# Second score pass of two attention layers on all 128 array rows, with a new table of priorities

## The chip, the cores and the metric

One core of a Trainium2 chip runs the whole program. The time is the device time of one execution in microseconds (us). The kernel before was timed three times: 1111.57, 1105.31 and 1106.12 us, median 1106.12 us.

## The reference

Four layers run one after the other on 512 tokens of 1024 channels, each as a pre-normalised residual: differential attention (layer 0), a gated causal convolution of 31 taps (layer 1), latent attention with a low-rank query and key (layer 2), differential attention again (layer 3). Cut to the scores, which the change touches:

```
# layers 0 and 3: 8 heads, two score maps (m = 0, 1) per head, 64 channels each
s = einsum('bhmqd,bhmkd->bhmqk', q[:, :, :, s0:e], k[:, :, :, :e]) * scale
p = chunk_causal_softmax(s, s0)
wts = p[:, :, 0] - lam * p[:, :, 1]
outs.append(einsum('bhqk,bhkd->bhqd', wts, v[:, :, :e]))
# layer 2: 8 heads, 128 channels without rotation and 64 rotated ones, the rotated key shared by all heads
s = (einsum('bhqd,bhkd->bhqk', qn[:, :, s0:e], kn[:, :, :e])
     + einsum('bhqr,bkr->bhqk', qr[:, :, s0:e], k_rope[:, :e])) * scale
```

Queries are taken in four blocks of 128 tokens, and block j sees the keys of blocks 0 to j.

## The kernel before

**Precision.** Every large product is made of float32r passes. An operand is split exactly into a high and a low part, and a product is the sum of high by high, high by low and low by high (`mm3`, three matmuls into the same PSUM bank).

**Scores of layers 0 and 3.** A map has only 64 channels, so one 128-row plane holds the high part of the query on one half of the partitions and its low part on the other (`stack`). The key tile has five planes of 512 tokens: 0 and 1 are the query's for m = 0 and 1, 2 and 3 hold the high part of the key of m = 0 and 1, copied to both halves, and plane 4 holds the low parts, that of m = 0 on the first 64 partitions, that of m = 1 on the last 64. A score block is then two passes: a first with 128 rows, (high and low query) by high key, and a second with the 64 rows of one half, high query by low key. Where the query block sees fewer than 256 keys, 256 are computed.

**Scores of layer 2.** Three passes with 128 rows for the unrotated channels, one with 128 rows for the rotated ones by the high key, and one with 64 rows for the rotated ones by the low key. The rotated key already stands on both halves of the partitions, its high and its low part.

**Around a score block.** VectorE masks it and takes the row maximum, ScalarE takes the exponential, TensorE transposes the weights (`wtr`), ScalarE copies them out (`wt`), TensorE multiplies them with V (`o`). One head follows the other; the projections of the next heads (`qk_a`, `v_a`, `g_a`, `q_a`, `kv_a`) and the output projection (`o` from `o_w` and `y`) stand between them on TensorE.

**Making a head ready (layers 0 and 3).** TensorE transposes query and key (`qk_tr`), ScalarE casts them into the head's tile `st` (six casts of 64 partitions), VectorE subtracts to get the low parts (four subtractions of 64 partitions).

**What sets the order.** The program is recorded as nodes, one engine each. `Plan.order` takes them by a list schedule: for each engine the node that could start first by estimated costs, ties by priority. Priority is the place in the program, shifted by the table `SHIFT` (one number for each section and engine) and by `AS` for attention. Buffers are slots counted in `SLOTS` and PSUM tiles are granted while the order is made. Each engine then runs its list strictly in that order, with semaphore waits. All loads are issued by SyncE.

In names of the profile the numbers are left out (`L_qk_st` is `L0_qk3_st1`, for example), so layers 0 and 3 share names.

Of the kernel before, what the change touches and what calls it, by code (L numbers as in the profile page):

```python
# [248 lines left out]
L1_ab6_w.pool=-54 L1_ab6_w_r.sp=4 L1_c0.dve=672 L1_c1.dve=701 L1_c3.dve=765 L1_c5.dve=1250 L1_c7.pe=185
L1_cq2.act=741 L1_cq2.pool=293 L1_cq4.act=-380 L1_cq4.pool=-367 L1_cs0.act=-348 L1_cs5.act=60 L1_cs6.act=-31  # L250
L1_cs7.act=3 L1_ct2_.act=94 L1_ct4_.act=-5138 L1_ctr0.act=123 L1_ctr0.pe=4634 L1_ctr1.act=-1571 L1_ctr1.pe=566
L1_ctr2.act=494 L1_ctr2.pe=492 L1_ctr3.act=809 L1_ctr3.pe=24 L1_ctr4.act=-1038 L1_ctr4.pe=-1038 L1_ctr5.act=852
# [1300 lines left out]
```

## Time and profile before

| | |
|---|---|
| median of three runs | 1106.12 us (1105.31 to 1111.57) |
| profiled execution, first to last instruction | 1108.7 us |
| TensorE matmul busy | 1065.0 us (96%), 5089 instructions |
| TensorE weight load busy | 847.5 us (76%) |
| VectorE busy | 813.3 us (73%) |
| ScalarE busy | 623.6 us (56%) |
| GpSimd busy | 209.5 us (19%) |
| DMA | 78.16 MB, mean 70 GB/s |

The page shows no time of its own for the profiled execution beside its span. A matmul's busy time reaches from its start to a modelled end and overlaps with the next, so "busy" on TensorE is not the same as productive: how far apart the starts of successive matmuls are says more. In rows of the trace, "64\*128" after the operation is rows by columns of the array that were used, and "128x512" is the moving operand. The layers lie at about 0 to 323, 323 to 556, 556 to 810 and 810 to 1109 us.

### The profile page before, as it was taken

What the parts mean: (1) busy time and instruction counts of PE and PEld (TensorE: products, weight loads), DVE (VectorE), ACT (ScalarE), POOL (GpSimd) and SP (SyncE); (2) the same over time, 40 slices, a digit from 0 to 9 for tenths busy, and PEclk for the clock granted to TensorE, in tenths of its full rate; (3) what the DMA queues carried; (4) which work ended last, traced back from release to release, by engine and by line L of the source; (5) the groups of instructions that cost most, each with busy time, mean ns of one, the idle gap of its engine ahead of it and who ended that gap; (6) DMA issues with size and microseconds to landing.
All of it is one profiled execution on the core that took longest, in us unless ns stands there. A gap on an engine that the chain in (4) does not pass through costs nothing.

```text
span 1108.7 us, 15142 instructions
## 1 busy us (share of the span) xinstructions
PE 1065.0 (96%) x5089; PEld 847.5 (76%) x5089; DVE 813.3 (73%) x2271; ACT 623.6 (56%) x1319; POOL 209.5 (19%) x133
## 2 busy tenths in 40 slices
PE   8899999999998998898999999999999999999898
PEld 6777877777686786686888877888887787777677
DVE  3876688888754999988555878874775588878771
ACT  6466366657654355796444676654435645667652
POOL 2400000000027499985520000000300000000000
PEclk9999999999999998999999999999999999999899
DMA  7231220302013322202231311011423121212002
GB/s 225 78 94 58 77 77 20 117 22 95 20 39 114 113 78 76 69 1 92 56 109 46 93 53 39 20 56 58 136 93 94 59 77 58 79 55 77 1 20 76
DMA packets 67254, 78.16 MB, mean 70 GB/s; under 512 B 15813, under 2 KB 44741, under 8 KB 67176
## 3 DMA queue, kind: packets, MB, share of 16 engines
q1 hardware_dynamic: 67176, 77.19, 22.7%
q8 instruction: 40, 0.66, 0.2%
q14 instruction: 38, 0.31, 0.1%
HBM read 75.08 MB, written 2.10 MB: 70 GB/s over the span
## 4 chain that ended last, share of the span: by engine, by line
PE 82%; DVE 5%; ACT 4%; POOL 3%; issue 2%; DMA 1%; SPq 1%; POOLq 0%; DVEq 0%; ACTq 0%
PE L_o L451 20%; PE L_qk_a L451 14%; PE L_g_a L451 13%; PE L_v_a L451 8%; PE L_ab_a L451 5%; PE L_c L451 2%; POOL L_cq L502 2%; POOL L_sqs L502 1%; PE L_q_a L451 1%; PE L_h6j_sc L451 1%; PE L_h1j_sc L451 1%; PE L_h5j_sc L451 1%; PE L_h4j_sc L451 1%; PE L_h7j_sc L451 1%; PE L_h3j_sc L451 1%
## 5 line engine op out<-in xcount | busy, mean ns | idle before, releaser
L451 PE MATMUL L_qk_a<-L_qk_w,Hh 128*128 128x512 f32 x512 | 164.1, 401 | 2.7 <-ACT Hh L481 1.9
L451 PE MATMUL L_o<-L_y,L_o_w 128*128 128x512 f32 x576 | 141.9, 397 | 1.2 <-DVE L_y L499 1.0
L502 POOL TENSOR_TENSOR L_sqs<-L_sqs,L_sq 128x512 f32<-128x512 f32 x28 | 44.2, 1579 | 513.2 <-DMA L_lay<-c_q_norm_g 275.9
L451 PE MATMUL L_g_a<-L_g_w,Hh 128*128 128x512 f32 x384 | 123.8, 404 | 0.7 <-DVE L_c_v L514 0.6
L451 PEld LDWEIGHTS L_o<-L_y,L_o_w 128*128 128x128 f32 x576 | 105.4, 188 | 24.3 <-DVE L_y L499 1.4
L451 PEld LDWEIGHTS L_qk_a<-L_qk_w,Hh 128*128 128x128 f32 x512 | 92.4, 188 | 24.0 <-ACT Hh L481 2.3
L506 DVE SCALAR_TENSOR_TENSOR L_c<-L_u,L_tab,L_c 128x512 f32<-128x512 f32 x150 | 102.8, 746 | 0.3
L451 PE MATMUL L_qk_a<-L_qk_w,Hl 128*128 128x512 f32 x256 | 100.3, 392 | 1.3 <-DVE Hl L506 1.3
L451 PE MATMUL L_ab_a<-Hh,L_ab_w 128*128 128x512 f32 x256 | 81.7, 397 | 0.7 <-DVE L_u L499 0.7
L451 PE MATMUL L_v_a<-L_v_w,Hh 128*128 128x512 f32 x256 | 81.7, 400 | 0.0
L451 PEld LDWEIGHTS L_g_a<-L_g_w,Hh 128*128 128x128 f32 x384 | 68.5, 189 | 16.9 <-issue 2.0
L502 POOL TENSOR_TENSOR L_cq<-L_cq,L_ct 128x512 f32<-128x512 f32 x60 | 79.4, 1323 | 10.5 <-ACT L_ct L481 7.2
L451 PE MATMUL L_g_a<-L_g_w,Hl 128*128 128x512 f32 x192 | 75.2, 392 | 0.0
L488 ACT CAST L_qk_st<-L_qk_tr 64x512 fp32r<-64x512 f32 x96 | 55.7, 580 | 15.5 <-PE L_qk_tr L457 14.3
L451 PEld LDWEIGHTS L_ab_a<-Hh,L_ab_w 128*128 128x128 f32 x256 | 48.8, 191 | 11.4 <-DVE L_u L499 1.1
L451 PEld LDWEIGHTS L_qk_a<-L_qk_w,Hl 128*128 128x128 f32 x256 | 48.1, 188 | 12.0 <-DVE Hl L506 1.7
L481 ACT ACTIVATE L_ct<-L_u,L_tab 128x512 f32<-128x512 f32 x60 | 43.0, 719 | 23.5 <-POOL L_cq L502 23.3
L451 PEld LDWEIGHTS L_v_a<-L_v_w,Hh 128*128 128x128 f32 x256 | 46.2, 188 | 10.0 <-issue 0.9
L451 PE MATMUL L_ab_a<-Hl,L_ab_w 128*128 128x512 f32 x128 | 50.6, 395 | 1.4 <-DVE Hl L506 1.4
L488 ACT CAST L_qk_w<-L_qk_w_r 128x1024 fp32r<-128x1024 f32 (+1 forms) x33 | 34.2, 1039 | 31.1 <-PE L_qk_a L451 15.3
L451 PE MATMUL L_g_a<-Hh,L_g_w 128*128 128x512 f32 x128 | 46.1, 415 | 5.4 <-POOL L_g_w L502 2.6
L451 PE MATMUL L_o<-L_o_w,L_y 128*128 128x512 f32 (+1 forms) x216 | 50.5, 379 | 0.5 <-DVE L_y L506 0.5
(376 smaller groups left out, 2387.1 us busy)
## 6 DMA issues: line engine op xcount, KB each, us to landing
L_qk_w_r<-a_w_in SPq DMA_DIRECT2D x62, 256.0 KB, 3.0
L_v_w_r<-a_w_in SPq DMA_DIRECT2D x16, 512.0 KB, 3.7
L_g_w_r<-a_w_in SPq DMA_DIRECT2D x16, 512.0 KB, 3.7
L_o_w_r<-a_w_out SPq DMA_DIRECT2D x16, 512.0 KB, 3.5
L_ab_w_r<-b_w_in SPq DMA_DIRECT2D x24, 256.0 KB, 3.0
L_g_w_r<-b_w_in SPq DMA_DIRECT2D x8, 512.0 KB, 3.7
L_o_w_r<-b_w_out SPq DMA_DIRECT2D x8, 512.0 KB, 3.5
L_g_w_r<-c_w_in SPq DMA_DIRECT2D x8, 512.0 KB, 3.6
```

Of the source, the lines that this page charges most:

```text
L451: lambda nc: nc.tensor.matmul(out.real(), a.real(), b.real(), start=start, stop=stop),
L481: nc.scalar.activation(out.real(), src.real(), func, scale=scale.real() if isinstance(scale, View) else scale, **kw)
L488: lambda nc: nc.scalar.copy(out.real(), src.real()), [src], [out])
L502: lambda nc: nc.gpsimd.tensor_tensor(out=out.real(), in0=a.real(), in1=b.real(), op=op), [a, b], [out])
L506: self.add("dve", out.n / 960.0 + (0.13 if isinstance(scalar, View) else 0.068), lambda nc: nc.vector.scalar_tensor_tensor(out=out.real(), ...
```

## The change

The second score pass of layers 0, 2 and 3 uses all 128 rows: the whole query plane (high and low part) by the low part of the key, which now stands on both halves of the partitions. It adds the product low by low, which was left out before. In layers 0 and 3 the low parts of the two maps get a plane each (tile `qk` with six planes instead of five, four slots), and two ScalarE copies of 64 partitions per head bring each low part to the other half. In layer 2 only the index changes. The number of matmuls and their moving sizes stay.

`build` asks for a DMA scratch of 1024 instead of the default. In the planner the estimated cost of a matmul is a little larger, and VectorE instructions whose operands all lie in SBUF are reckoned to be held up by a busy GpSimd (`port`). The table of priorities is another one: 875 entries instead of 883, most numbers differ. Comments are gone. The new table reorders every engine's list.

```diff
 SLOTS = {
...
-    "qk": (4, [P, 5, 512], F32R, True),
+    "qk": (4, [P, 6, 512], F32R, True),
...
 SHIFT = {k: int(v) for k, v in (x.split("=") for x in """
...
-L3_ytr3.pe=-303 L3_ytr4.pe=-121 L3_ytr5.pe=-9 L3_ytr6.pe=167 L3_ytr7.pe=6 none.act=677 none.dve=-72
...
+L3_ytr2.pe=-50 L3_ytr3.pe=-23 L3_ytr4.pe=-2546 L3_ytr5.pe=-630 L3_ytr7.pe=-46 none.act=3426 none.dve=28
 """.split())}
...
     def mm(self, out, a, b, start, stop):
...
-        self.add("pe", max(cyc / 2400.0, 0.213 if a.buf.dtype == F32 else 0.027) + 0.0025,
+        self.add("pe", 0.218 if a.buf.dtype == F32 else max(cyc / 2400.0 + 0.013, 0.109),
...
         else:
+            self.port(out, src, 2)
             self.add("dve", self._dve2x(out, src), lambda nc: nc.vector.tensor_copy(out.real(), src.real()), [src], [out])
...
+    def port(self, a, b, kind=1):
+
+        self.shares = 0 if a.buf.psum or b.buf.psum else kind
...
                     est = max(f, n.ready, st)
+                    if n.port == 2:
+                        est = max(est, free["pool"])
...
             cost = n.cost
+            if n.port == 1:
+                cost += min(cost, max(0.0, free["pool"] - est))
...
                         for m, rows in enumerate(HALVES):
                             for to in HALVES:
                                 p.copy(st[to, 2 + m, :], tr[rows, :])
                         for m, rows in enumerate(HALVES):
-                            p.tt(st[rows, 4, :], tr[rows, :], st[rows, 2 + m, :].f32(), ALU.subtract)
+                            p.tt(st[rows, 4 + m, :], tr[rows, :], st[rows, 2 + m, :].f32(), ALU.subtract)
+                        for m, rows in enumerate(HALVES):
+                            p.copy(st[HALVES[1 - m], 4 + m, :], st[rows, 4 + m, :].f32())
...
-                    rows, qs = HALVES[m], slice(jb * P, (jb + 1) * P)
+                    qs = slice(jb * P, (jb + 1) * P)
                     with p.only_when(bufs=[pb]), p.group("pe"):
                         self.mm(sc[:, 0:n], st[:, m, qs], st[:, 2 + m, 0:n], True, False)
-                        self.mm(sc[:, 0:n], st[rows, m, qs], st[rows, 4, 0:n], False, True)
+                        self.mm(sc[:, 0:n], st[:, m, qs], st[:, 4 + m, 0:n], False, True)
...
         def attend_(h):
             st, rt = heads[h]
-            rows, m = HALVES[h % 2], h % 2
+            m = h % 2
...
                     self.mm(o, rt[:, m, qs], lat[0][:, 3, 0:n], False, False)
-                    self.mm(o, rt[rows, m, qs], lat[1][rows, 3, 0:n], False, True)
+                    self.mm(o, rt[:, m, qs], lat[1][:, 3, 0:n], False, True)
...
 def build(shapes):
-    nc = bacc.Bacc("TRN2", target_bir_lowering=False, num_devices=1)
+    nc = bacc.Bacc("TRN2", target_bir_lowering=False, num_devices=1, dynamic_dma_scratch_size=1024)
```

The order that comes out of the new table is shown at the two places that the prediction speaks of. First TensorE at the end of layer 3, from the transposes of the last two heads' keys (`L3_qk3_tr01`, `L3_qk3_tr11`) to the first scores of head 6 (`L3_h6j0_sc0`). Before:

```order
L457 MATMUL L3_qk3_tr01_9812<-ident_109,L3_qk3_T_9293 128x128 x4
L457 MATMUL L3_qk3_tr11_9824<-ident_109,L3_qk3_T_9293 128x128 x4
L457 MATMUL L3_h5j2_wtr_9831<-ident_109,L3_h5j2_p_9701 128x128 x3
L451 MATMUL L3_o5_9787<-V_114,L3_h5j2_wt_9832 128x128 x3
L451 MATMUL L3_h6j0_sc0_9846<-L3_qk3_st0_9487 128x256 x2
L451 MATMUL L3_h6j0_sc1_9850<-L3_qk3_st0_9487 128x256 x2
L457 MATMUL L3_h5j3_wtr_9867<-ident_109,L3_h5j3_p_9747 128x128 x4
```

And changed, the same stretch:

```order
L457 MATMUL L3_qk3_tr01_9816<-ident_109,L3_qk3_T_9313 128x128 x4
L451 MATMUL L3_o02_9729<-L3_o0_w0_9590,L3_y0_9784 128x512 x3
L457 MATMUL L3_qk3_tr11_9833<-ident_109,L3_qk3_T_9313 128x128 x4
L457 MATMUL L3_ytr3_9841<-ident_109,V_114 128x128 x4
L451 MATMUL L3_o01_9718<-L3_o0_w0_9590,L3_y0_9784 128x512 x3
L451 MATMUL L3_o03_9738<-L3_o0_w0_9590,L3_y0_9784 128x512 x3
L451 MATMUL L3_o00_9708<-L3_o0_w0_9590,L3_y0_9784 128x512 x3
L457 MATMUL L3_h5j2_wtr_9865<-ident_109,L3_h5j2_p_9693 128x128 x3
L451 MATMUL L3_h6j0_sc0_9872<-L3_qk3_st0_9612 128x256 x2
L451 MATMUL L3_o5_9808<-V_114,L3_h5j2_wt_9866 128x128 x3
L451 MATMUL L3_h6j0_sc1_9889<-L3_qk3_st0_9612 128x256 x2
```

Twelve passes of the output projection and four transposes of finished heads (`L3_ytr3`) now stand between the key's transposes and the first score of head 6; before there were only the transposes and products of head 5.

Second, ScalarE at the same place. The casts fill the tiles of head 6 (`L3_qk3_st0`) and head 7 (`L3_qk3_st1`) from the transposed keys. Before:

```order
L488 CAST L3_qk3_st0_9487<-L3_qk3_tr01_9812 64x512 x4
L488 COPY L3_h5j2_wt_9832<-L3_h5j2_wtr_9831 128x384
L488 CAST L3_qk3_st1_9495<-L3_qk3_tr11_9824 64x512 x3
L481 ACTIVATE L3_h5_osq_9799,L3_h5_oss_9798<-L3_o5_9787 128x128
L488 CAST L3_qk3_st1_9495<-L3_qk3_tr11_9824 64x512
```

And changed:

```order
L488 CAST L3_qk3_st0_9612<-L3_qk3_tr01_9816 64x512 x4
L481 ACTIVATE L3_y1_9794<-L3_ytr3_9841,L3_lay_4918 128x512
L488 CAST L3_qk3_st1_9644<-L3_qk3_tr11_9833 64x512
L488 CAST L3_qk3_st0_9612<-L3_qk3_st0_9612 64x512
L488 CAST L3_qk3_st1_9644<-L3_qk3_tr11_9833 64x512 x2
L488 CAST L3_qk3_st0_9612<-L3_qk3_st0_9612 64x512
L488 COPY L3_h5j2_wt_9866<-L3_h5j2_wtr_9865 128x384
L488 CAST L3_qk3_st1_9644<-L3_qk3_tr11_9833 64x512
```

The two new copies of head 6 (`st0` from `st0`) stand among the casts of head 7, and the copy-out of head 5's transposed weights (`L3_h5j2_wt`) stands behind them.

More of the change, by code (lines that the diff above doesn't have):

```diff
@@ L191 @@
     __slots__ = ("eng", "cost", "emit", "deps", "succ", "left", "bufs", "prio", "seq", "ready", "start", "end",
-                 "dma", "table", "label")
+                 "dma", "table", "label", "port")
     def __hash__(self):
@@ L249 @@
[L249 to L252, printed above, removed]
-L1_ctr5.pe=443 L1_ctr6.act=1041 L1_ctr6.pe=928 L1_ctr7.act=35 L1_ctr7.pe=936 L1_cw7.act=-3440 L1_cw7.dve=-374
@@ new lines @@
+L0_h0_oss.dve=-46 L0_h0_ov.dve=963 L0_h0_p.act=-14833 L0_h0_p.dve=530 L0_h0_sc.pe=-4834 L0_h0_wt.act=-1323
+L0_h0_wtr.pe=26 L0_h1_mx.dve=-2 L0_h1_or_y.dve=-3025 L0_h1_osq.act=1796 L0_h1_ov.dve=693 L0_h1_p.act=-9029
+L0_h1_p.dve=1045 L0_h1_sc.dve=265 L0_h1_sc.pe=-311 L0_h1_wt.act=-4 L0_h1_wtr.pe=-292 L0_h2_cf.dve=448
+L0_h2_mx.dve=-1387 L0_h2_or_y.dve=2129 L0_h2_osq.act=-1195 L0_h2_oss.dve=-8105 L0_h2_ov.dve=-485 L0_h2_p.act=579
+L0_h2_p.dve=-5549 L0_h2_sc.dve=2135 L0_h2_sc.pe=-157 L0_h2_wt.act=-6662 L0_h2_wtr.pe=8 L0_h3_cf.dve=1197
@@ new lines @@
+L0_h3_mx.dve=-11983 L0_h3_or_y.dve=2 L0_h3_osq.act=139 L0_h3_oss.dve=-245 L0_h3_p.act=-4374 L0_h3_p.dve=-517
+L0_h3_sc.dve=-1955 L0_h3_sc.pe=1655 L0_h3_wt.act=43 L0_h3_wtr.pe=-193 L0_h4_cf.dve=-1967 L0_h4_mx.dve=4
+L0_h4_or_y.dve=1800 L0_h4_osq.act=-2373 L0_h4_oss.dve=7442 L0_h4_ov.dve=-286 L0_h4_p.dve=333 L0_h4_sc.dve=-366
+L0_h4_sc.pe=377 L0_h4_wt.act=-4720 L0_h4_wtr.pe=-371 L0_h5_mx.dve=-2544 L0_h5_or_y.dve=-1251 L0_h5_osq.act=407
+L0_h5_oss.dve=-2342 L0_h5_ov.dve=-270 L0_h5_p.act=-2332 L0_h5_p.dve=1087 L0_h5_sc.dve=-102 L0_h5_sc.pe=-118
@@ new lines @@
+L0_o03.pe=2240 L0_o0_w.act=-14701 L0_o0_w_r.sp=-99 L0_o1.dve=-2976 L0_o1.pe=46158 L0_o10.dve=3145 L0_o10.pe=18314
+L0_o11.dve=377 L0_o11.pe=26161 L0_o12.dve=539 L0_o12.pe=172 L0_o13.dve=10887 L0_o13.pe=696 L0_o1_w.act=11677
+L0_o1_w.dve=-18423 L0_o1_w_r.sp=2477 L0_o2.dve=-1968 L0_o4.pe=12397 L0_o5.pe=108 L0_o6.dve=67 L0_o6.pe=229
+L0_o7.dve=-1834 L0_o7.pe=193 L0_qk0_T.dve=-892 L0_qk0_a.pe=11920 L0_qk0_sq.act=151 L0_qk0_ss.dve=-16196
+L0_qk0_st.act=-253 L0_qk0_st.dve=962 L0_qk0_t.dve=-893 L0_qk0_tr.pe=-2029 L0_qk0_v.dve=171 L0_qk0_w.act=1203
@@ new lines @@
+L0_qk0_w.dve=-5262 L0_qk0_w_r.sp=2191 L0_qk0_y.dve=-5155 L0_qk1_T.dve=4020 L0_qk1_a.pe=1331 L0_qk1_sq.act=17016
+L0_qk1_ss.dve=835 L0_qk1_st.act=3130 L0_qk1_st.dve=195 L0_qk1_t.dve=768 L0_qk1_tr.pe=12905 L0_qk1_v.dve=34650
+L0_qk1_w.act=2731 L0_qk1_w_r.sp=20 L0_qk1_y.dve=-49 L0_qk2_T.dve=1802 L0_qk2_a.pe=10091 L0_qk2_ss.dve=4913
+L0_qk2_st.act=-1534 L0_qk2_st.dve=-5329 L0_qk2_t.dve=-19274 L0_qk2_tr.pe=1063 L0_qk2_v.dve=92 L0_qk2_w.act=-5042
+L0_qk2_w.dve=3143 L0_qk2_w_r.sp=3403 L0_qk2_y.dve=3359 L0_qk3_T.dve=-26 L0_qk3_a.pe=3302 L0_qk3_sq.act=517
@@ new lines @@
+L2_h3_mx.dve=593 L2_h3_p.act=2318 L2_h3_sc.dve=-476 L2_h3_sc.pe=-20 L2_h3_wt.act=-1964 L2_h3_wtr.pe=2879
+L2_h4_mx.dve=-1083 L2_h4_p.act=8545 L2_h4_sc.dve=5322 L2_h4_sc.pe=1976 L2_h4_wt.act=-13859 L2_h4_wtr.pe=160
+L2_h5_mx.dve=2725 L2_h5_sc.pe=14252 L2_h5_wt.act=158 L2_h6_p.act=-5038 L2_h6_sc.dve=1995 L2_h6_wt.act=-20
+L2_h6_wtr.pe=180 L2_h7_mx.dve=1480 L2_h7_p.act=5 L2_h7_sc.dve=-8188 L2_h7_sc.pe=-1250 L2_h7_wtr.pe=-4099
+L2_kv0_T.dve=-1231 L2_kv0_a.act=80 L2_kv0_a.pe=-12 L2_kv0_ss.dve=3308 L2_kv0_w.act=-124 L2_kv0_w.dve=-4600
@@ new lines @@
+L2_kv0_w_r.sp=-1402 L2_kv0_y.dve=1821 L2_kv1_T.dve=669 L2_kv1_a.act=932 L2_kv1_a.pe=-929 L2_kv1_sq.act=-2020
+L2_kv1_ss.dve=255 L2_kv1_v.dve=-2438 L2_kv1_w.act=74 L2_kv1_w.dve=4482 L2_kv1_w_r.sp=-126 L2_kv1_y.dve=19
+L2_kv2_T.act=-370 L2_kv2_T.dve=-1561 L2_kv2_a.act=-55 L2_kv2_a.pe=915 L2_kv2_sq.act=195 L2_kv2_ss.dve=2822
+L2_kv2_v.dve=-1210 L2_kv2_w.act=1956 L2_kv2_w.dve=3406 L2_kv2_w_r.sp=534 L2_kv2_y.dve=-1632 L2_kv3_T.act=-309
+L2_kv3_a.pe=1438 L2_kv3_sq.act=887 L2_kv3_ss.dve=-124 L2_kv3_v.dve=-586 L2_kv3_w.act=1362 L2_kv3_w.dve=1801
@@ new lines @@
+L2_kv3_w_r.sp=380 L2_l0.dve=-11353 L2_l1.dve=519 L2_l2.dve=579 L2_l3.dve=-1800 L2_l4.dve=7995 L2_l5.dve=-182
+L2_l6.dve=-12 L2_l7.dve=3955 L2_lat0.act=3869 L2_lay.act=-45 L2_lay.dve=-2 L2_ltr0.pe=-22 L2_ltr1.pe=-529
+L2_ltr2.pe=63 L2_o0.dve=357 L2_o0.pe=1784 L2_o00.dve=-319 L2_o00.pe=4165 L2_o01.dve=-413 L2_o01.pe=6111
+L2_o02.dve=-1114 L2_o03.dve=4 L2_o03.pe=6808 L2_o0_w.dve=22554 L2_o0_w_r.sp=18967 L2_o1.dve=-7474 L2_o1.pe=6268
+L2_o10.dve=-988 L2_o10.pe=-10132 L2_o11.dve=810 L2_o11.pe=1764 L2_o12.dve=1882 L2_o12.pe=2125 L2_o13.dve=1623
@@ new lines @@
+L2_o13.pe=-2 L2_o1_w.act=3120 L2_o1_w.dve=-233 L2_o1_w_r.sp=599 L2_o2.dve=2239 L2_o3.dve=924 L2_o3.pe=1039
+L2_o4.dve=354 L2_o4.pe=2728 L2_o5.dve=155 L2_o5.pe=1240 L2_o6.dve=-283 L2_o6.pe=5 L2_o7.dve=-726 L2_o7.pe=-601
+L2_p0_rt.act=1360 L2_p0_rt.dve=-41 L2_p0_st.act=18120 L2_p0_st.dve=8699 L2_p0_tr.pe=-19814 L2_p1_rt.act=-388
+L2_p1_rt.dve=-161 L2_p1_rtr.pe=1364 L2_p1_st.act=-17 L2_p1_st.dve=-2349 L2_p2_rt.act=-529 L2_p2_rt.dve=13272
+L2_p2_rtr.pe=-530 L2_p2_st.act=-897 L2_p2_st.dve=2574 L2_p2_tr.pe=-13699 L2_p3_rt.act=-886 L2_p3_rt.dve=-15618
@@ new lines @@
+L2_p3_rtr.pe=-1001 L2_p3_st.act=4 L2_p3_st.dve=221 L2_p3_tr.pe=66 L2_q0_T.act=2238 L2_q0_T.dve=1124 L2_q0_a.pe=-2742
+L2_q0_sq.act=2248 L2_q0_ss.dve=298 L2_q0_t.dve=-5303 L2_q0_v.dve=-28 L2_q0_w.act=18805 L2_q0_w.dve=-50
+L2_q0_w_r.sp=1011 L2_q0_y.dve=2840 L2_q1_T.act=14428 L2_q1_T.dve=2100 L2_q1_a.pe=3109 L2_q1_sq.act=2658
+L2_q1_ss.dve=9566 L2_q1_t.dve=24164 L2_q1_v.dve=-1183 L2_q1_w.act=51 L2_q1_w.dve=1724 L2_q1_y.dve=-85
+L2_q2_T.act=-75232 L2_q2_T.dve=12189 L2_q2_a.pe=-1070 L2_q2_sq.act=8 L2_q2_ss.dve=313 L2_q2_t.dve=6159 L2_q2_w.act=17
@@ new lines @@
+L2_ytr3.pe=-14 L2_ytr4.pe=-4475 L2_ytr5.pe=-7400 L2_ytr6.pe=1353 L3_g0_a.act=1182 L3_g0_a.pe=-2667 L3_g0_w.act=30
+L3_g0_w.dve=8 L3_g0_w_r.sp=1342 L3_g1_a.act=15 L3_g1_w.act=702 L3_h0_cf.dve=2070 L3_h0_mx.dve=257 L3_h0_or_y.dve=1542
+L3_h0_osq.act=17191 L3_h0_oss.dve=901 L3_h0_ov.dve=8124 L3_h0_p.act=-1515 L3_h0_p.dve=6 L3_h0_sc.dve=6
+L3_h0_wt.act=633 L3_h1_cf.dve=-21 L3_h1_mx.dve=-15218 L3_h1_or_y.dve=10 L3_h1_osq.act=14029 L3_h1_oss.dve=23
+L3_h1_ov.dve=-3124 L3_h1_p.act=-2 L3_h1_p.dve=-7490 L3_h1_sc.dve=1288 L3_h1_sc.pe=-496 L3_h1_wt.act=885
@@ new lines @@
+L3_h1_wtr.pe=-1371 L3_h2_cf.dve=-2894 L3_h2_mx.dve=474 L3_h2_or_y.dve=-3906 L3_h2_osq.act=-5480 L3_h2_oss.dve=54
+L3_h2_p.act=-759 L3_h2_p.dve=-2 L3_h2_sc.dve=-1128 L3_h2_sc.pe=-206 L3_h2_wtr.pe=-3587 L3_h3_cf.dve=-1310
+L3_h3_mx.dve=30605 L3_h3_or_y.dve=22331 L3_h3_osq.act=90 L3_h3_oss.dve=-546 L3_h3_ov.dve=1193 L3_h3_p.act=893
+L3_h3_sc.dve=-6800 L3_h3_sc.pe=-2 L3_h3_wt.act=6926 L3_h3_wtr.pe=2 L3_h4_cf.dve=997 L3_h4_mx.dve=37
+L3_h4_or_y.dve=7887 L3_h4_osq.act=-17958 L3_h4_oss.dve=555 L3_h4_ov.dve=-22625 L3_h4_p.act=1910 L3_h4_p.dve=16791
@@ new lines @@
+L3_h4_sc.dve=-2 L3_h4_sc.pe=-243 L3_h4_wt.act=-3 L3_h4_wtr.pe=-207 L3_h5_cf.dve=-124 L3_h5_mx.dve=5740
+L3_h5_or_y.dve=1807 L3_h5_osq.act=264 L3_h5_oss.dve=-69 L3_h5_ov.dve=6556 L3_h5_p.act=621 L3_h5_p.dve=845
+L3_h5_sc.dve=-6 L3_h5_sc.pe=-1784 L3_h5_wt.act=1077 L3_h5_wtr.pe=-91 L3_h6_cf.dve=177 L3_h6_mx.dve=-19386
+L3_h6_or_y.dve=72 L3_h6_osq.act=6 L3_h6_oss.dve=1868 L3_h6_ov.dve=-10307 L3_h6_p.act=-4003 L3_h6_p.dve=-75
+L3_h6_sc.dve=1044 L3_h6_sc.pe=-5986 L3_h6_wt.act=-261 L3_h6_wtr.pe=-2451 L3_h7_cf.dve=49 L3_h7_mx.dve=-1167
@@ new lines @@
+L3_o5.pe=-120 L3_o6.dve=-3 L3_o6.pe=2137 L3_o7.dve=180 L3_o7.pe=-5399 L3_ot000.act=-876 L3_ot000.sp=-233
+L3_ot010.act=-5426 L3_ot010.sp=-39 L3_ot020.act=-2308 L3_ot020.sp=1913 L3_ot030.act=95 L3_ot030.sp=-637
+L3_ot100.sp=-3003 L3_ot110.sp=-2749 L3_ot120.act=375 L3_ot120.sp=-2783 L3_ot130.act=-2196 L3_ot130.sp=44
+L3_ot13256.act=-813 L3_ot13256.sp=3327 L3_qk0_T.dve=-633 L3_qk0_a.pe=-8719 L3_qk0_ss.dve=4389 L3_qk0_st.act=-11926
+L3_qk0_st.dve=-375 L3_qk0_t.dve=-624 L3_qk0_tr.pe=-4 L3_qk0_v.dve=-1913 L3_qk0_w.act=229 L3_qk0_w.dve=-551
@@ L357, in __init__ @@
         self.shift = 0
+        self.shares = 0
         self.guard = []
@@ L391, in _new @@
         n.eng, n.cost, n.emit, n.deps, n.bufs = eng, 0.0, [], set(), set()
-        n.succ, n.dma, n.table = [], None, None
+        n.succ, n.dma, n.table, n.port = [], None, None, 0
         n.label = None
@@ L421, in add @@
         n.emit.append(emit)
+        n.port = max(n.port, self.shares)
+        self.shares = 0
         n.label = n.label or next((v.buf.name for v in list(writes) + list(reads) if v.buf.tag), 'none')
@@ L497, in tt @@
         if eng == "dve":
+            self.port(a, b)
             self.add("dve", out.n / 960.0 + 0.068,
@@ L513, in ts @@
         kw = {} if op1 is None else {"op1": op1}
+        self.port(out, a, 2)
         self.add("dve", self._dve2x(out, a) + 0.062 * (len(rd) - 1), lambda nc: nc.vector.tensor_scalar(
```

202 lines of the change are left out of this document (70 added, 132 removed).

## The prediction

> **What bounds the kernel now.** I read the head of the page first, then the busy time of each layer, then the longest pieces of the chain that ended last.
>
> ```profile
> span 1108.7 us, 15142 instructions
> PE 1065.0 (96%) x5089; PEld 847.5 (76%) x5089; DVE 813.3 (73%) x2271; ACT 623.6 (56%) x1319; POOL 209.5 (19%) x133
> ```
>
> ```profile
> 0.00:323.00 323.00, 311.62 (x1473) 241.33 (x1474) 235.14 (x741) 191.05 (x432) 21.02 (x18) 1.00 0.25 76
> 323.00:556.00 233.00, 213.82 (x936) 173.00 (x935) 190.34 (x309) 131.98 (x213) 170.47 (x105) 0.96 0.26 78
> 556.00:820.00 264.00, 258.69 (x1342) 214.40 (x1341) 188.01 (x562) 141.66 (x320) 18.02 (x11) 0.99 0.22 66
> 820.00:1109.00 289.00, 280.84 (x1344) 218.79 (x1342) 199.85 (x661) 158.86 (x355) 0.00 (x0) 0.98 0.20 63
> ```
>
> ```profile
> 539.47 17.05 PE L_o L451 x75
> 788.94 21.76 PE L_qk_a L451 x96
> ```
>
> The four rows are layers 0 to 3; after the length come PE, weight load, DVE, ACT and POOL busy, then the granted clock. TensorE has work almost always: it idles 11.4, 19.2, 5.3 and 8.2 us. So a nanosecond that TensorE's queue loses is mostly lost to the whole. But a busy row doesn't say what a pass costs; distances of starts do. The chain's long runs give the clean price of a 512-column pass: 17.05/75 and 21.76/96, both 0.227 us. Now a place where the second score pass stands among such passes, matmuls first, weight loads below.
>
> ```profile
> 226.71 0.39 PE L451 MATMUL L_g_a<-L_g_w,Hl 128*128 128x512 f32 x1
> 226.94 0.59 PE L451 MATMUL L_h5j_sc<-L_qk_st 128*128 128x256 f32 x2
> 227.46 0.73 PE L451 MATMUL L_g_a<-L_g_w,Hh 128*128 128x512 f32 x2
> 228.03 0.40 PE L451 MATMUL L_g_a<-L_g_w,Hl 128*128 128x512 f32 x1
> 228.26 0.59 PE L451 MATMUL L_h5j_sc<-L_qk_st 128*128 128x256 f32 x2
> ```
>
> ```profile
> 226.71 0.19 PEld L451 LDWEIGHTS L_h5j_sc<-L_qk_st 128*128 128x128 f32 x1
> 227.15 0.18 PEld L451 LDWEIGHTS L_h5j_sc<-L_qk_st 64*128 64x128 f32 x1 [0.25 <-issue]
> 227.46 0.30 PEld L451 LDWEIGHTS L_g_a<-L_g_w,Hh 128*128 128x128 f32 x2
> ```
>
> ```profile
> 645.31 0.52 PE L451 MATMUL L_h0j_sc<-L_p_st 128*128 128x256 f32 x3
> 645.67 0.59 PE L451 MATMUL L_h0j_sc<-L_lat,L_p_rt 128*128 128x256 f32 x2
> 646.18 1.65 PE L451 MATMUL L_kv_a<-L_kv_w,L_lat 128*128 128x512 f32 x6
> 647.67 0.52 PE L451 MATMUL L_h0j_sc<-L_p_st 128*128 128x256 f32 x3
> ```
>
> Three 256-column passes with 128 rows go from 645.31 to 645.67, so 0.12 us each, though each has its own weights. From 226.94 to 228.26 lie two score passes and three projection passes: 2 x 0.12 + 3 x 0.227 = 0.92 us of work in 1.32 us, 0.40 too much. From 645.31 to 647.67 lie five score passes and six projection passes: 0.60 + 1.36 = 1.96 in 2.36, again 0.40. Nobody is waited for there. The 64-row load starts only 0.25 us after the load before it ended, put down to "issue", and the next 128-row load starts only after 0.31 us more (227.15 to 227.46): the queue stops both when the height used changes to 64 and when it changes back.
>
> **The change part by part.** How many such passes there are is read from their weight loads, first and last of eight rows each:
>
> ```profile
> L451 PEld LDWEIGHTS L_h0j_sc<-L_qk_st 64*128 64x128 f32 x16 | 2.9, 183 | 3.9 <-issue 3.4 <-DVE L_qk_st L499 0.2
> L451 PEld LDWEIGHTS L_h7j_sc<-L_qk_st 64*128 64x128 f32 x16 | 2.9, 183 | 3.8 <-issue 3.3
> L451 PEld LDWEIGHTS L_h0j_sc<-L_lat,L_p_rt 64*128 64x128 f32 x4 | 0.7, 183 | 0.9 <-issue 0.6
> L451 PEld LDWEIGHTS L_h7j_sc<-L_lat,L_p_rt 64*128 64x128 f32 x4 | 0.7, 183 | 0.9 <-issue 0.6
> ```
>
> 8 x 16 in layers 0 and 3 together, 8 x 4 in layer 2: 160 passes, each between 128-row work. *Removed:* 160 x 0.40 = 64 us, some 26 each in layers 0 and 3 and 13 in layer 2. *Added on TensorE:* nothing; a pass of 128 rows with the same columns takes the 0.12 us already counted.
>
> [...]
>
> *Added on ScalarE:* two copies of 64x512 per head, 32 in all. From SBUF with 64 rows none is in the trace; the nearest rows:
>
> ```profile
> L488 ACT CAST L_qk_st<-L_qk_tr 64x512 fp32r<-64x512 f32 x96 | 55.7, 580 | 15.5 <-PE L_qk_tr L457 14.3
> L488 ACT CAST L_y<-L_yv 128x512 fp32r<-128x512 f32 x8 | 4.7, 616 | 2.3 <-DVE L_yv L499 2.3
> ```
>
> Between 0.58 and 0.62; I take 0.62, which reads SBUF: 20 us, ten per layer, on an engine busy 191 of 323 and 159 of 289 us. In most places that lies under projections. Without cover a head's first score comes 1.24 us later, at most 16 x 1.24 = 20 us. The cover is thinnest at the end of layer 3:
>
> ```profile
> 1031.05 0.65 PE L457 MATMUL L_qk_tr<-ident,L_qk_T 128*128 128x128 f32 x4 [1.04 <-ACT L_h5j_p L481]
> 1034.64 1.65 PE L451 MATMUL L_o<-V,L_h5j_wt 128*128 128x128 f32 x6 [1.24 <-ACT L_h5j_wt L488]
> 1039.14 1.12 PE L457 MATMUL L_h5j_wtr<-ident,L_h5j_p 128*128 128x128 f32 x4 [1.11 <-ACT L_h6j_p L481]
> ```
>
> ```profile
> 1031.74 2.35 ACT L488 CAST L_qk_st<-L_qk_tr 64x512 fp32r<-64x512 f32 x4 [0.17 <-PE L_qk_tr L457]
> 1034.11 0.48 ACT L488 COPY L_h5j_wt<-L_h5j_wtr 128x384 f32<-128x384 f32 x1
> 1034.49 1.76 ACT L488 CAST L_qk_st<-L_qk_tr 64x512 fp32r<-64x512 f32 x3
> ```
>
> Here TensorE waits for ScalarE, which runs through. The new order puts both copies of head 6 and a cast ahead of head 5's copy-out, and twelve passes (2.7 us) on TensorE over them. I take the copies as covered, but of the 16 passes of heads 6 and 7 (6.4 us) only half as gained where ScalarE is the later one: 3 us back.
>
> *The other engines* keep their work while the time shrinks.
>
> ```profile
> 645.00:700.00 55.00, 51.82 (x293) 41.47 (x292) 46.14 (x178) 37.37 (x103) 0.00 (x0) 0.97 0.11 36
> 700.00:755.00 55.00, 54.49 (x317) 43.69 (x316) 42.13 (x140) 31.80 (x83) 0.00 (x0) 1.00 0.15 48
> 250.00:323.00 73.00, 69.82 (x345) 53.19 (x345) 53.22 (x186) 47.10 (x118) 1.59 (x2) 1.00 0.15 44
> ```
>
> In layer 2's attention VectorE works 88.3 of 110 us; with 13 gone it is 88.3 of 97, or 91%, and some stalls must come: I give 2 back there, and 1 at the end of layer 0 (53.2 of 73 us, with the heads 6 and 7 in it). The bounds of these give-backs are nothing and all that those stretches gain (13 and 6 us).
>
> VectorE's own list of work doesn't change: the two subtractions per head that make the key's low parts only write to other planes.
>
> *The table, the scratch, the sixth plane.* Every list is new. In the layers without scores TensorE idles 19.2 us, and the changed planner knows better what GpSimd costs VectorE; whether that gains or loses can't be read from an order. I take nothing, with 10 us either way. The smaller scratch and the larger tile I cost at nothing. Whether a load uses the scratch at all no row shows, but nearly all packets (67176 of the page's 67254) go by the hardware queue, and the 16 engines are taken up by it for 22.7% of the span, so that even loads that took half as long again would find room:
>
> ```profile
> q1 hardware_dynamic: 67176, 77.19, 22.7%
> ```
>
> Sum: 1108.7 - 64 + 3 + 2 + 1 = 1050.7 on the profiled execution, which lies 2.6 above the median of the runs. Against the median: **1048 us**.
>
> **The rivals.**
> - *Chains of other engines take the gain in the heads* (11%). Layer 2's 32 passes, and heads 6 and 7 of layers 0 and 3 with 32, gain nothing, since VectorE and ScalarE are the later ones: 64 x 0.40 = 26 us less gain, and the copies of those four heads come in the open, 5 us: 1106 - 64 + 31 = 1073. For it: the waits at 1031 to 1039. Against: "issue" is all that stands before the 64-row loads nearly everywhere.
> - *The new table also closes gaps* (6%). Of the 30.6 us of idle TensorE in layers 0 and 1 half goes: 1048 - 15 = 1033.
> - *The change doesn't do what it says* (3%): the stop belongs to any load whose rows are in use, so that the second pass's load and that of the pass behind it come in the open as before, 0.19 + 0.19 in place of 0.40: a gain of 160 x 0.02 = 3 us, 1103. Against: the passes from 645.31 all use the same rows, each with a load of its own, and keep 0.12 us. [...]
> - *Slower* (2%): the new table leaves TensorE waiting in every query block between scores and transposes, as here once:
>
> ```profile
> 300.80 0.55 PE L457 MATMUL L_h7j_wtr<-ident,L_h7j_p 128*128 128x128 f32 x3 [1.22 <-ACT L_h7j_p L481]
> ```
>
> 64 blocks in layers 0 and 3 by 1.22 = 78 us: 1106 - 64 + 78 = 1120. It decides from 1 us per block on (64/64). Against: the list of the changed kernel has projections between most scores and transposes.
>
> **How the numbers follow.** The forecast has 78%, with a range of its own from 1036 (nothing given back, 6 us, and as much from the table) to 1060 (the table takes its 10, and 2 more are given back). It reaches toward the first two rivals, to 1034 and 1068, and leaves out the rest of them. Within 1%, 1095 to 1117, lies the third rival, beyond it the fourth; 1% is about what a measurement of this kernel can tell from no change. Faster 95%, same 3%, slower 2%.
>
> **What would show it.** In the changed profile no score pass has 64\*128, and the idle before score loads put down to "issue" is near nothing. A score pair among projections takes 0.24 us: the same window arithmetic must leave nothing over. TensorE instructions stay about 5089, and ScalarE gets 32 casts of L_qk_st from itself at about 0.6 us. VectorE's and ScalarE's shares rise (to about 78% and 61%). Wrong would be: 128-row second passes still 0.3 us apart from the next; or TensorE's idle time, 43.7 us before, grown by more than 20, with waits for ScalarE or VectorE in the heads.

## The result and the profile after

The changed kernel takes 1070.49 us (median of four runs, 1068.59 to 1075.12), the kernel before in the same session 1106.45 us (1105.31 to 1111.57): a ratio of 0.967, with a 95% interval of 0.964 to 0.970. It is 36 us faster where 58 were forecast, and lies just outside the range of 1034 to 1068. One of the four executions of the kernel without a SiLU below took 2026.39 us, twice the other three, and is left out of its time and ratio.

The head of the page of the changed kernel, and the first line of its chain of waits:

```profile
span 1066.7 us, 15176 instructions
PE 1012.0 (95%) x5089; PEld 840.0 (79%) x5089; DVE 806.8 (76%) x2271; ACT 642.1 (60%) x1351; POOL 209.2 (20%) x133
...
PE 60%; DVE 16%; ACT 12%; issue 5%; POOL 5%; DMA 1%; SPq 1%; DVEq 0%; ACTq 0%; POOLq 0%
```

Before, the same line of the chain read:

```profile
PE 82%; DVE 5%; ACT 4%; POOL 3%; issue 2%; DMA 1%; SPq 1%; POOLq 0%; DVEq 0%; ACTq 0%
```

So TensorE holds 60% of the chain instead of 82%, and VectorE and ScalarE together 28% instead of 9%. First what was removed: a score pair among projections, and the weight loads of both score passes in two heads of layers 0 and 3, and of the rotated channels in one head of layer 2.

```profile
1020.12 0.86 PE L451 MATMUL L_o<-L_o_w,L_y 128*128 128x512 f32 x3
1020.82 0.40 PE L451 MATMUL L_h7j_sc<-L_qk_st 128*128 128x256 f32 x2
1021.05 0.86 PE L451 MATMUL L_o<-L_o_w,L_y 128*128 128x512 f32 x3
```

```profile
L451 PEld LDWEIGHTS L_h7j_sc<-L_qk_st 128*128 128x128 f32 x32 | 5.3, 188 | 1.1 <-ACT L_h7j_wt L488 0.3 <-ACT L_h7j_p L481 0.2
L451 PEld LDWEIGHTS L_h0j_sc<-L_qk_st 128*128 128x128 f32 x32 | 5.3, 188 | 2.7 <-ACT L_h0j_p L481 1.4 <-PE L_qk_a L451 0.6 <-ACT L_qk_st L488 0.2
L451 PEld LDWEIGHTS L_h7j_sc<-L_lat,L_p_rt 128*128 128x128 f32 x8 | 1.4, 188 | 0.1
```

The two passes take 1021.05 - 1020.82 = 0.23 us, with nothing left over; no score load has 64 rows, and the idle put down to "issue" (3.0 to 3.6 us in each of the eight such rows of layers 0 and 3 before) is gone from these rows. The stops are removed.

What came instead stands in the longest waits of TensorE (engine, instruction, who is waited for: total us, times, longest):

```profile
PE L_ytr L457 <- DVE V L522: 6.9, 1, 6.9
PE L_ctr L457 <- POOL L_cq L504: 5.6, 1, 5.6
PE L_ytr L457 <- ACT L_h5j_p L481: 4.6, 1, 4.6
PE L_qk_a L451 <- DVE Hl L513: 3.8, 1, 3.8
PE L_h2j_wtr L457 <- ACT L_h2j_p L481: 2.6, 1, 2.6
```

Before, the longest single wait was this one:

```profile
PE L_Rtr L451 <- DVE L_Rdg L514: 3.2, 1, 3.2
```

To see all of it, not only the longest, I take the ends of all 5089 matmuls of a trace and subtract from each distance between two ends the clean distance for that size (0.227 us for 512 columns, 0.175 for 384, 0.118 for 256, 0.110 for 128, found as the usual distances where nothing waits). The clean distances sum to 968.5 us in every kernel here. What is left over at a change between 64 and 128 rows, up to 0.2 us each, is counted as *stop*, the rest as *wait* (it also holds what passes lose while the granted clock is halved: 512 columns then take 0.427 us, 128 columns 0.213, by the traces before and after):

```
            stop  wait = start   L0    L1    L2    L3
before      62.1  73.2    8.8  12.5  28.7  11.5  11.6
changed      0    93.4   10.1  21.7  23.9  18.4  19.3
```

The gain of the span, 1108.7 - 1066.7 = 42 us, is 62 us of stops less 20 us of new waits: 9 in layer 0, 7 in layer 2, 8 in layer 3, 1 at the start, and 5 fewer in layer 1.

The clock is not behind these 20 us: both traces have 31 us at half the granted clock before the last matmul. Whether a wait costs more than its length isn't shown: in the traces before and after, each of the eleven stretches at half clock before the last matmul (3.4 to 13.7 us) begins within 7 us of a wait of TensorE of more than 1.1 us, but that the wait brings it on isn't tested.

### The profile page after: what moved, and what is told of

It reads as the page before. It is cut to its first block, busy times and chain, and to the rows that moved or that the text cites. A ratio compares the mean times of both kernels' runs of the same rounds, so it can differ in the third digit from the quotient of the medians.

```text
span 1066.7 us, 15176 instructions
## 1 busy us (share of the span) xinstructions
PE 1012.0 (95%) x5089; PEld 840.0 (79%) x5089; DVE 806.8 (76%) x2271; ACT 642.1 (60%) x1351; POOL 209.2 (20%) x133
## 4 chain that ended last, share of the span: by engine, by line
PE 60%; DVE 16%; ACT 12%; issue 5%; POOL 5%; DMA 1%; SPq 1%; DVEq 0%; ACTq 0%; POOLq 0%
PE L_o L451 18%; PE L_g_a L451 12%; PE L_qk_a L451 10%; PE L_v_a L451 6%; ACT L_qk_st L488 3%; DVE L_c L513 3%; POOL L_cq L504 3%; PE L_ab_a L451 2%; POOL L_sqs L504 1%; PE L_c_a L451 1%; ACT G L481 1%; PE L_ytr L457 1%; DVE L_qk_T L501 1%; DVE L_qk_st L501 1%; SPq L545 1%
## 5 line engine op out<-in xcount | busy, mean ns | idle before, releaser
L451 PE MATMUL L_g_a<-L_g_w,Hh 128*128 128x512 f32 x384 | 120.1, 394 | 0.3 <-ACT V L481 0.3
L488 ACT CAST L_g_w<-L_g_w_r 128x1024 fp32r<-128x1024 f32 x32 | 33.6, 1053 | 36.9 <-PE L_v_a L451 23.3
L501 DVE TENSOR_TENSOR L_qk_st<-L_qk_tr,L_qk_st 64x512 fp32r<-64x512 f32 x64 | 44.1, 688 | 15.2 <-ACT L_qk_st L488 13.9
L481 ACT ACTIVATE L_ct<-L_u,L_tab 128x512 f32<-128x512 f32 x60 | 43.2, 721 | 19.8 <-POOL L_cq L504 19.3
L501 DVE TENSOR_TENSOR L_qk_w<-L_qk_w_r,L_qk_w 128x1024 fp32r<-128x1024 f32 (+1 forms) x30 | 35.4, 1182 | 22.0 <-ACT L_qk_w L488 21.6
```

The lines of the kernel that those rows point to most:

```text
L451: lambda nc: nc.tensor.matmul(out.real(), a.real(), b.real(), start=start, stop=stop),
L481: nc.scalar.activation(out.real(), src.real(), func, scale=scale.real() if isinstance(scale, View) else scale, **kw)
L488: lambda nc: nc.scalar.copy(out.real(), src.real()), [src], [out])
L501: lambda nc: nc.vector.tensor_tensor(out=out.real(), in0=a.real(), in1=b.real(), op=op), [a, b], [out])
```

## The experiments

The change has three parts that can be separated: the height of the second pass, the 32 copies on ScalarE, and the new order. My first theory: the stops are gone in full and the order or the copies bring the waits (*Table* and *Copies* in the expectations). The rival, *Pace*: the other engines set the pace of the heads, so that without the stops TensorE must wait in any order. Where a diff below has `alt`, only the operands of the instruction that is issued change; the planner still sees the old ones, so every engine keeps its list.

**Height alone, in the order before.**

```diff
-self.mm(sc[:, 0:n], st[rows, m, qs], st[rows, 4, 0:n], False, True)
+self.mm(sc[:, 0:n], st[rows, m, qs], st[rows, 4, 0:n], False, True,
+        alt=(st[:, m, qs], st[:, 4, 0:n]))
```

(and likewise in layer 2). Plane 4 holds the low part of one map's key on each half.

> The kernel before with its order unchanged on every engine; only the second score passes read all 128 rows: in layer 2 as in the change, in layers 0 and 3 the whole plane that holds the low parts of both maps, so that the low query of one map by the low key of the other is added to the scores. No copies, no sixth plane, old table. The stop of 0.40 us at 160 passes goes in every theory (62 to 64 us). Pace (with TensorE quicker, the chains of the other engines come last in any order): about 20 to 26 us of new waits, 1064 to 1070. Table (the new order makes the waits): the old order keeps its waits, 1044 to 1050. Copies (the 32 ScalarE copies make the waits): also 1044 to 1050.

Measured: 1050.97 us, ratio 0.949 (0.945 to 0.953).

```profile
span 1051.1 us, 15142 instructions
PE 1004.4 (96%) x5089; PEld 838.5 (80%) x5089; DVE 811.1 (77%) x2271; ACT 622.5 (59%) x1319; POOL 209.4 (20%) x133
```

The stops go from 62.1 to 0, the waits from 73.2 to 77.6. So nearly all of the stops' time is realised if nothing else moves; the other engines do not set the pace. This version is 57 us faster than the kernel before and beats the changed kernel by about 20: copies, sixth plane and table aren't needed for it, since what it adds, low query of one map by low key of the other, is again a product of two low parts.

**The new order with 64-row second passes.**

```diff
-self.mm(sc[:, 0:n], st[:, m, qs], st[:, 4 + m, 0:n], False, True)
+self.mm(sc[:, 0:n], st[:, m, qs], st[:, 4 + m, 0:n], False, True,
+        alt=(st[rows, m, qs], st[rows, 4 + m, 0:n]))
```

> The changed kernel with its order unchanged on every engine, its copies too; only the second score passes use the 64 rows of one half again. Pace: the stops come back where TensorE now waits for others, so only about 62 - 20 = 42 us come back: 1106 to 1115. Table: the order's waits stay beside the stops, 1070 + 62 = 1132. Copies: between them, since the second pass still waits for the copies, about 1120 to 1132.

Measured: 1120.75 us, ratio 1.012 (1.009 to 1.015). The stops are back (62.0), the waits fall from 93.4 to 83.5: the stops had hidden 10 us of them. The time lies at the lower edge of what *Copies* gave (1120 to 1132), above *Pace* and below *Table*. The new order with the old height is thus 1.2% slower than the kernel before.

**The whole edit with the planner and the table of before.**

> The whole edit of the scores (128 rows, six planes, copies, small scratch) with the old table of priorities and the old planner. Pace: 1064 to 1072, like the changed kernel. Table: 1044 to 1052, some 20 below the changed kernel. Copies: about 1070.

Measured: 1151.27 us, ratio 1.039 (1.036 to 1.043), stops 0, waits 176.5, of which 74.5 in layer 3. All three theories had put it at 1044 to 1072 and missed: with 32 nodes more the same table gives a bad order. It says nothing of the copies' own price. Nor are all these waits the order's alone. Layer 3 with the height alone, then layer 3 here and a stretch of it (after the busy times of five engines comes the granted clock, then DMA):

```profile
754.00:1051.00 297.00, 285.94 (x1489) 239.73 (x1487) 219.95 (x690) 168.86 (x368) 5.69 (x4) 1.00 0.22 70
```

```profile
792.00:1149.00 357.00, 312.72 (x1489) 254.24 (x1488) 227.10 (x690) 182.74 (x385) 5.78 (x4) 0.90 0.19 58
1074.00:1118.00 44.00, 24.67 (x80) 17.45 (x80) 17.46 (x75) 11.54 (x35) 0.00 (x0) 0.50 0.00 1
```

The trace runs 133 us at half clock before the last matmul, that with the height alone 24. Half of the difference, 55 us, is the most that the clock can have cost of the 99 us more waits (an estimate: TensorE also idles in these stretches).

**The new order without the copies.** The two subtractions write plane 4, the second pass reads it, the 32 copies issue nothing.

```diff
+p.last.emit = []      # after each of the 32 copies
```

> The changed kernel with its order unchanged, without the 32 ScalarE copies: the low parts of both maps share a plane again, and the 128-row second pass of layers 0 and 3 adds the low query of one map by the low key of the other. Pace and table: 1066 to 1071, as before the copies went. Copies: 1050 to 1055, as their 20 us and the longer way to a head's first score go.

Measured: 1065.93 us, ratio 0.963 (0.960 to 0.966). Without them the changed kernel is 4.6 us faster, so that is about what the copies cost in the new order; the intervals of the two ratios still overlap. The same instructions as in the first experiment, in the new order, take 15 us more.

**The old table's order (1151 us) without the copies.**

> The run with the whole edit under the old table (1151) with its order unchanged on every engine, without the 32 ScalarE copies; the 128-row second pass of layers 0 and 3 adds the low query of one map by the low key of the other, as in the first run. If the copies themselves made that run slow, this falls to the 1051 of the first run, at most 1065. If the order did (a table of numbers fitted to another list of nodes), it stays at 1135 to 1150.

Measured: 1148.12 us, ratio 1.036 (1.032 to 1.040). The difference of 3 us lies within the intervals; the order, with the slow clock that comes with it (granted 0.95 in its trace, 0.94 with the copies), is what is bad, not the copies.

**The copies in the order before.** The first experiment with the sixth plane, and the 32 copies put into ScalarE's list where their operand is ready; nothing else moves.

> The first run (old order, 128-row second passes, 1051) with the sixth plane and the 32 copies put into ScalarE's list where their operand is ready by the planner's reckoning, before the next node there; every other instruction keeps its place. Copies cheap in a good order (they cost 4.6 us in the new order): 1053 to 1060. Copies dear because they come between the casts and the copies-out that TensorE waits for: 1065 to 1075, which would make the changed kernel's time theirs.

Measured: 1068.52 us, ratio 0.963 (0.960 to 0.966): 17.5 us more than with the height alone (16.5 by the ratios), and as fast as the changed kernel. Waits rise by 9.0 in layer 0 and 8.9 in layer 3, where the copies are, by about 1 in layer 2, and fall by some 4 in layer 1. The smaller DMA scratch and the sixth plane came in with the copies and weren't run alone; the 62 weight loads of 256 KB land in 3.0 us (median) with them and without. Up to 7 of the 17.5 us can be clock, half of the difference between 38 us at half clock in this trace and 24 with the height alone. Rows of TensorE in layer 0:

```profile
142.61 0.28 PE L453 MATMUL L_h2j_sc<-L_qk_st 128*128 128x256 f32 x1
143.64 0.51 PE L453 MATMUL L_h2j_sc<-L_qk_st 128*128 128x256 f32 x2 [0.75 <-ACT L_qk_st L682]
144.76 0.39 PE L453 MATMUL L_h2j_sc<-L_qk_st 128*128 128x256 f32 x1 [0.62 <-ACT L_qk_st L682]
```

L682 is the inserted copy. It looks as if the price were this wait of the second pass; the next run asks whether it is.

**The same copies, read by nobody.** They stay at their places in ScalarE's list, but write a plane of their own, and the second pass reads plane 4.

```diff
-alt=(st[:, m, qs], st[:, 4 + m, 0:n]))
+alt=(st[:, m, qs], st[:, 4, 0:n]))
-eout=st[rows, 4 + m, :])
+eout=st[rows, 4, :])
-p.late.append((p.last, st, st[HALVES[1 - m], 4 + m, :], st[rows, 4 + m, :].f32()))
+p.late.append((p.last, st, st[HALVES[1 - m], 5, :], st[rows, 4, :].f32()))
```

> The order of before with the 32 copies at the same places of ScalarE's list as in the kernel with copies in the old order, but the second score pass reads one plane with the low parts of both maps, which VectorE alone writes, and nothing reads what the copies write. The second pass then adds low query of one map by low key of the other, a product far below the last digit that counts. Two theories of the 17.5 us that the copies cost in the old order. Waiting: the second pass and what stands behind it on TensorE wait for the copies; then nearly all of it goes, 1051 to 1055 us. Occupation: ScalarE's 20 us of copies push back its casts, exponentials and copy-outs, which TensorE waits for anyway; then the time stays at 1066 to 1069. Anything between divides the cost between the two.

Measured: 1068.0 us, ratio 0.964 (0.959 to 0.970), waits 93.3 against 93.1. The waits for L682 are gone and nothing is gained. The price is ScalarE's time: what stands behind a copy in its list is late. It is the copies' own time, for ScalarE idles 1.3 us in all ahead of the 32 of them:

```profile
L682 ACT CAST L_qk_st<-L_qk_st 64x512 fp32r<-64x512 f32 x32 | 19.8, 618 | 1.3 <-DVE L_qk_st L502 0.7
```

In the trace of this kernel, TensorE and then ScalarE:

```profile
195.40 0.40 PE L453 MATMUL L_qk_a<-L_qk_w,Hl 128*128 128x512 f32 x1
196.75 0.94 PE L453 MATMUL L_o<-V,L_h3j_wt 128*128 128x128 f32 x6 [0.94 <-ACT L_h3j_wt L490]
198.00 1.16 PE L453 MATMUL L_o<-V,L_h3j_wt 128*128 128x128 f32 x8 [0.32 <-ACT L_h3j_wt L490]
```

```profile
195.14 1.05 ACT L490 CAST L_g_w<-L_g_w_r 128x1024 fp32r<-128x1024 f32 x1
196.21 0.48 ACT L490 COPY L_h3j_wt<-L_h3j_wtr 128x384 f32<-128x384 f32 x1
196.72 0.62 ACT L682 CAST L_qk_st<-L_qk_st 64x512 fp32r<-64x512 f32 x1
197.36 0.59 ACT L490 COPY L_h3j_wt<-L_h3j_wtr 128x512 f32<-128x512 f32 x1
197.97 0.62 ACT L682 CAST L_qk_st<-L_qk_st 64x512 fp32r<-64x512 f32 x1
```

And the same place with the height alone:

```profile
191.05 0.40 PE L452 MATMUL L_qk_a<-L_qk_w,Hl 128*128 128x512 f32 x1
191.28 1.79 PE L452 MATMUL L_o<-V,L_h3j_wt 128*128 128x128 f32 x14
```

ScalarE runs through from cast to copy-out to copy, one copy of 0.62 us stands ahead of the second copy-out, and two others, at 192.20 and 193.31, stood among the casts ahead of the first. TensorE, which ran its 14 matmuls in one go, waits twice. The engine is busy only 60% of the span, but not here.

**All score passes of layers 0 and 3 with 64 rows**, in the order before: does the stop belong to each 64-row pass or to the change of height? (The product of the query's low part and the key's high part is left out.)

```diff
-self.mm(sc[:, 0:n], st[:, m, qs], st[:, 2 + m, 0:n], True, False)
+self.mm(sc[:, 0:n], st[:, m, qs], st[:, 2 + m, 0:n], True, False,
+        alt=(st[rows, m, qs], st[rows, 2 + m, 0:n]))
```

> The kernel before with its order unchanged; in layers 0 and 3 the first score pass, too, reads only the 64 rows of one half (high query by high key; the low query by high key is left out). 256 passes with 64 rows in 92 unbroken runs, in place of 128 passes each alone. If the stop belongs to the change of height: 92 round trips in place of 128, 36 x 0.40 = 14 us less, about 1092. If it belongs to each pass with 64 rows: 128 more of them, 51 us more, about 1157. If a change from one half to the other stops too, between 1092 and 1106.

Measured: 1086.39 us, ratio 0.980 (0.976 to 0.983). There are now 256 passes of 64 rows in layers 0 and 3 where there were 128, and they stand in 92 stretches. 58 of these hold two passes of one score block and cost 0.40 us each (median) over the clean distances, about as much as one pass alone did before. So the stop belongs to the change of height. The 32 stretches of four cost only 0.09 us (median), for a reason that the last section gives; counted with that, the stops of the two layers fall from 49.9 to 27.4 us. One stretch of four, its weight loads and those around it:

```profile
142.84 0.19 PEld L452 LDWEIGHTS L_qk_a<-L_qk_w,Hl 128*128 128x128 f32 x1
143.40 0.41 PEld L452 LDWEIGHTS L_h2j_sc<-L_qk_st 64*128 64x128 f32 x4 [0.37 <-ACT L_v_w L489]
143.94 0.30 PEld L452 LDWEIGHTS L_qk_a<-L_qk_w,Hh 128*128 128x128 f32 x2
```

The load waits 0.37 us ahead of the stretch, and its four loads then take 0.41 us in all: no stop inside. The profile puts this one down to ScalarE, not to "issue"; the place and the length are those of the stop. Going to 64 rows and back cost 62.1/160 = 0.39 us in the kernel before.

**One of the new waits taken away.** The wait of 4.6 us in layer 3 of the changed kernel (`ytr` for `h5j_p`), ScalarE's rows there:

```profile
985.75 1.28 ACT L481 ACT_TABLE_LOAD   x1
987.05 1.91 ACT L481 ACTIVATE G<-G 128x2048 f32<-128x2048 f32 x1
988.97 1.28 ACT L481 ACT_TABLE_LOAD   x1
990.27 0.67 ACT L481 ACTIVATE L_h5j_p<-L_h5j_sc,L_h5j_mx,L_rq 128x384 f32<-128x384 f32 x1
```

The new list puts a SiLU of the gate between exponentials of head 5, and with it two table loads: 4.5 us. I replaced that SiLU by a plain copy.

> The changed kernel with its order unchanged; the SiLU of the second gate chunk of layer 3 is a plain copy, so the gate there is left without its SiLU and ScalarE loads no tables around it. If the longest wait of layer 3 (4.57 us before two transposes, put down to the exponential of head 5) is the two table loads and the SiLU ahead of that exponential in ScalarE's list, it falls by about 2.6 us (two loads of 1.28) to 2.0 us. If it is something else, it stays.

> The same kernel as the single look without the SiLU of layer 3's second gate chunk (a plain copy in its place, so the gate is not computed there), timed. If the wait of 4.6 us before the transposes of y was worth its length, the ratio to the kernel before falls from 0.967 by 2.8 to 4.6 us of 1107, to 0.963 to 0.965. If the wait is handed on to the next instruction that VectorE is late with, it stays at 0.966 to 0.968.

Measured: 1075.08 us in one execution, and 1070.85 us as the median of three, ratio 0.966 (0.962 to 0.971): no gain that can be told, though the interval also covers a gain of the wait's full length. Layer 3's waits, 18.9 instead of 19.3 us by the trace, speak for none. TensorE there, in the changed kernel and then without the SiLU:

```profile
991.09 1.97 PE L457 MATMUL L_ytr<-ident,V 128*128 128x128 f32 x8 [4.57 <-ACT L_h5j_p L481]
992.85 1.49 PE L451 MATMUL L_o<-V,L_h5j_wt 128*128 128x128 f32 x6
```

```profile
989.42 0.66 PE L457 MATMUL L_ytr<-ident,V 128*128 128x128 f32 x4 [1.72 <-ACT L_h5j_p L481]
990.25 0.66 PE L457 MATMUL L_ytr<-ident,V 128*128 128x128 f32 x4 [0.17 <-ACT L_h5j_p L481]
993.02 1.65 PE L451 MATMUL L_o<-V,L_h5j_wt 128*128 128x128 f32 x6 [2.12 <-DVE V L513]
```

The wait shrinks from 4.57 to 1.72 us as expected, and 2.12 us come up behind it for VectorE, which in the changed kernel was done by then. This long wait isn't worth its length; the chain behind it is late as well.

All together (us; stop and wait as above; each ratio is to the kernel before as timed in the same session):

| kernel | time | ratio to before | stop | wait |
|---|---|---|---|---|
| before | 1106.45 | 1 | 62.1 | 73.2 |
| changed | 1070.49 | 0.967 | 0 | 93.4 |
| height alone, old order | 1050.97 | 0.949 | 0 | 77.6 |
| old order, with copies | 1068.52 | 0.963 | 0 | 93.1 |
| old order, copies not read | 1068.0 | 0.964 | 0 | 93.3 |
| new order, no copies | 1065.93 | 0.963 | 0 | 91.2 |
| new order, 64 rows | 1120.75 | 1.012 | 62.0 | 83.5 |
| all score passes 64 rows | 1086.39 | 0.980 | 39.6 | 73.9 |
| old table, whole edit | 1151.27 | 1.039 | 0 | 176.5 |
| old table, no copies | 1148.12 | 1.036 | 0 | 167.2 |
| changed, no SiLU in layer 3 | 1070.85 | 0.966 | 0 | 94.2 |

## Why the prediction was right and wrong

**Removed, 160 x 0.40 = 64 us: right.** 62.1 us by the trace, none left after, and 57 us of them in the time when nothing else moves. That the two passes then take 0.24 us was right too (0.23), and so was that the stop belongs to a change of height.

**The third rival**, a stop for any load whose rows are in use: fell. The 128-row loads of 0.188 us lie beside passes of the same height and a pair keeps 0.23 us.

**The steps that failed: the table taken at "nothing, with 10 us either way", and "I take the copies as covered".** With the height alone the kernel takes 1051 us where 1048 were forecast; the rest of the miss, 20 us, is these two terms. The new order costs 15 us, the same instructions compared (waits by layer: 8.5 more in layer 0, 5.4 in layer 2, 3.6 in layer 3, 3.5 fewer in layer 1): more than the 10 allowed, and not closing gaps but opening them. The copies cost 4.6 us in that order, and 17.5 in the old one, where they come close to the bound "without cover", 20 us, though by another way: I had priced a first score that comes later, and what comes later is everything behind the copies in ScalarE's list. Their duration was right (0.62 us; the page has 32 more ScalarE instructions), but I read the cover from ScalarE's share of a layer, 191 of 323 us, while the copies come in a bunch with the casts, copy-outs and exponentials of the same head. The two ways end at about the same time, 1068.5 and 1070.5 us. One may read the new order's 15 us as room that it leaves for the copies; that is argued, not shown. What GpSimd costs VectorE, which the changed planner reckons with, is seen in the kernel before: three subtractions of `L_v_w` (128x1024) from 31.07 take 6.29 us beside a busy GpSimd, the next, at 42.80 beside an idle one, 1.23 us. What the new order has of that reckoning wasn't run alone.

**Give-backs of 3 + 2 + 1 us: about right for what they priced.** They were for TensorE outrunning the other engines, and with the height alone the waits grow by 4.4. In the changed kernel they are too small, by the order and the copies: layer 2 was to give back 2 and gave 7, layer 0 gave 9 in place of 1, layer 3 gave 8 in place of 3. On the profiled execution the sum was 1050.7 and the span is 1066.7: 14 of the 16 us are new waits (20.2 where 6 were given), 2 the stops. The other 6 us against the median come from setting a span against a median: the span before lay 2.6 above its median, the changed kernel's lies 3.8 below.

**The first rival** (1073) was nearest in time, but not for its reason: it had the passes of layer 2 and of heads 6 and 7 gain nothing, and with the height alone they gain nearly in full. Of its terms only the smaller one, copies in the open (5 us), was there, 4.6 in this order; the larger part, the order's 15, it did not have.

**What would show it.** The 64-row passes, the idle at "issue", 5089 instructions and 32 casts came as said; VectorE is at 76% and ScalarE at 60% (78 and 61 said), because the kernel is longer than forecast. The sign for being wrong, TensorE's idle time grown by more than 20, was badly chosen: by the busy row it grew from 43.7 to 54.7, by the ends of matmuls the waits grew by 20. A matmul of 512 columns reads as busy for 0.39 us (226.71 in the kernel before) where the ends lie 0.227 us apart, which may hide short waits.

**Open.** Why the new order waits more in layers 0, 2 and 3. Single places can be named (the SiLU above), but taking that one away moved the wait on. An order for the height alone, from a table searched for it, wasn't tried.

## What to carry to other kernels

Cost an instruction that is added to an engine by that engine's list at the place where it goes in, not by its share of the layer: in the old order ScalarE, 59% busy without them, passed on nearly all of the copies' 20 us. A wait that the profile names isn't the price of its cause, so take the dependence away and keep the work (or the other way round) before you believe it. When an edit comes with a new order, run it in the old order first, part by part: here the smallest part alone was the best version.

## What was not expected of the hardware

Two 64-row passes in a row that use opposite halves of the array ran side by side in the kernel with all score passes at 64 rows: the second and third of the stretch shown above end at 143.899 and 143.902 us by their single records in the trace, 3 ns apart, where two 128-row passes of that size end 118 ns apart. In most of the 32 stretches of four, two pairs of passes end within 10 ns of each other. That is why the stops there come to 27.4 us and not to 92 x 0.39 = 36, and it is more than enough for the 6 us by which the kernel is faster than the 1092 expected. The two table loads shown in the changed kernel take 1.28 us each, and next to no time is lost beside them: the SiLU starts 0.02 us after the first load ends, the second load 0.01 us after the SiLU, and the exponential 0.02 us after the second load.
